# Delta-rule keys kept unnormalised: key norms in biases and factors, decays masked first and exponentiated per head, the first state product held back

## The chip, the cores and the metric

The kernel runs on one core of one Trainium2 chip. The metric is the device time of one execution in microseconds; three executions of the kernel before took 1210.19, 1213.13 and 1214.18 us, so its median is 1213.13 us. One execution was profiled: every duration below is from it, in microseconds from the start of its span. PE is the matrix engine, DVE the vector engine, ACT the scalar engine with the activation tables, POOL the GpSimd engine; SP issues all the transfers (DMAs) spoken of here.

## The reference, cut to what matters

A decoder block of width 1024 over 528 positions (16 learned ones, then 512): SwiGLU, a mixer, SwiGLU. The mixer has an attention branch and a gated delta rule with 8 heads of 64 keys and 64 values. The change touches the delta rule alone:

```python
q = l2norm(q) * (GDN_DK ** -0.5)
k = l2norm(k)                      # k * rsqrt(sum(k*k) + EPS), per position and head
beta = sigmoid(b_raw)
gc = cumsum(g)                     # g < 0: a decay per position and head
decay = exp(where(tri_incl, gc[:, None] - gc[None, :], -inf))
kb = k * beta
lmat = where(tri_strict, (kb @ k.T) * decay, 0)
tmat = inverse(eye + lmat)
u_c, w_c = tmat @ (v * beta), tmat @ (kb * exp(gc))
intra = (q @ k.T) * decay
# per chunk, with the state carried:
v_new = u - w @ state
o = (q * exp(gc)) @ state + intra @ v_new
state = state * exp(g_last) + (k * exp(g_last - gc)).T @ v_new
```

The kernels work on five chunks: chunk 0 is the 16 learned positions, chunks 1 to 4 have 128 positions each.

## The kernel before

All activations lie channels by positions. Weights are streamed by SP into three buffers, split by ACT (`whi`, L173) and DVE (`wlo`, L174) into a high and a low part, and multiplied in three passes (L188). The program is four stages one after the other: SwiGLU 1, the mixer's projections with the delta rule, the attention, SwiGLU 2. Within the mixer each part is given a priority (`At(slot)`), a scheduler puts the instructions of each engine into a fixed order by these, and `HOLD` (L67) adds orderings: an entry `(name, i, t, k)` lets the instructions marked `name, i` come only behind matmul `k` of projection `t`. Each engine then works strictly in its order, so that a waiting instruction holds up all behind it on that engine.

The delta rule's part, in the order in which the data flow:

- `rates` makes beta, the cumulative decays `gc` (token-major), `lb` = gc - log(1 + exp(-b)), that is gc + log(beta), and `kd` = exp(g_last - gc), and writes `gc` as rows to memory (`growd`).
- `k_tile` (four, one for two heads): projection, short convolution on DVE (three instructions L710), SiLU on ACT into `kT`, transposes on PE to token-major (`tok`, L723), and copies into `ktok` with sums of squares `ss`.
- `decay(c, True, n)`, called ahead of `k_norm`: the row of decays is broadcast to all partitions by a DMA, POOL subtracts it from `lb` (L782), POOL masks it (L783) and ACT exponentiates all eight heads in one instruction (L785, recorded at L147).
- `k_norm`: the norm `kn`, five multiplications of `ktok` by it (L747, DVE and POOL), 20 transposes back on PE (L750, `kback`), 20 ACT copies into `kT` (L752), and five multiplications of `ktok` by `kd` on POOL (L753).
- `lower(c)`: eight products of keys (L804, tile `kk`, in two PSUM buffers, the only two of their tag) times the decay on DVE (L806), then to memory (`ld`).
- `v_tile`, `q_tile`, `z_tile`: as `k_tile`; the products L761 and L1252 take beta into `bv`.
- `solve`: the inverse by forward substitution, 31 steps on DVE for chunks 1 to 4 (`lt`, `T`, `rk`, L827 and L829), 15 steps on POOL for chunk 0 (`meta`). `merge_meta` transposes the latter on DVE (L838) into `X[0]`; `merge` puts together the former.
- `scan(c)`: `vn` = X times the right-hand side, an ACT copy of it (L922), the state product `su` of `ktok` and `vn` (L926), and for c > 0 the outputs with `decay(c, False, P)`.

The projections for keys, values and queries (`qkv` in the rows), each of 48 matmuls, run on PE through all this, and their results leave PSUM through two buffers by a DVE instruction (L706, tile `cx`).

Of the kernel before, what the change touches and what calls it, by code (L numbers as in the profile page):

```python
# [41 lines left out]
NTAG = {"tA": 3, "tB": 3, "tC": 3, "tD": 4, "kb": 10, "rr": 1, "vn": 2, "m": 4}  # L42
# [6 lines left out]
    "rr": "rr", "vn": "vn", "m": "tb xt nz nz2 zs meta phm plm",  # L49
# [17 lines left out]
HOLD = (('nm', 0, 0, 32), ('nm', 1, 0, 36), ('b', 0, 1, 36), ('g', 0, 2, 42), ('tok', 1, 4, 5), ('tok', 2, 5, 4), ('tok', 3, 6, 2), ('back', 0, 8, 25), ('tok', 4, 8, 21), ('tok', 7, 10, 0), ('sq', 0, 11, 25), ('kvn', 0, 14, 12), ('kvn', 1, 14, 18))  # L67
# [25 lines left out]
def build(tc, a, out, tap=None):  # L93
# [3 lines left out]
    with ctx:  # L97
# [375 lines left out]
        # ---------------- feed-forward 1  # L473
# [42 lines left out]
        # ---------------- token mixer  # L516
# [91 lines left out]
        # ---- rates and decays, token-major  # L608
        def rates():
# [59 lines left out]
            nc.vector.tensor_tensor(out=lb, in0=gc, in1=lb, op=ALU.subtract)  # L669
            nc.vector.tensor_tensor(out=kd, in0=egl, in1=gc, op=ALU.subtract)  # L670
# [15 lines left out]
        eglp = one([P, 5, 4], "eglp")  # L686

# [13 lines left out]
        # ---- short convolution, token-major copies  # L701
# [33 lines left out]

        def k_norm(psm):
            pm = psm[0:NM].rearrange("p c x -> p (c x)")
            sq = tmp("tsq", SEQ, NM)
            nc.scalar.activation(sq, pm, AF.Square)
            nc.scalar.copy(ktok[0][0:NM], pm)  # L740
            nc.vector.tensor_reduce(out=ss[0:NM, 0], in_=hd(sq), axis=AX.X, op=ALU.add)
            rsqrt(kn, ss, 1.0)
            pst = sm_tile("psmk")
            for c in range(5):
                n, o = tlen(c), toff(c)
                kk = hd(ktok[c][0:n])
# [7 lines left out]
            tap("kT0", kT[0])  # L754

        def v_tile(i, psm):
# [3 lines left out]
            for c in range(1, 5):  # L760
                nc.vector.tensor_tensor(out=hd(bv[c][:, i * P:(i + 1) * P]), in0=hd(ps[:, c - 1]),  # L761
                                        in1=hb(beta[:, c, 2 * i:2 * i + 2], P, 2), op=ALU.mult)
# [11 lines left out]
        # ---- the triangular systems  # L774
        def decay(c, lower, n):
            if lower:
                t = b4("dec", [P, H, P]) if c else one([NM, H, NM], "L0")
            else:
                t = b4("dec", [P, H, P])
            dq.dma_start(t, growd[c, :, 0:n].partition_broadcast(n))  # L780
            gcb = (lb if lower else gc)[0:n, c].unsqueeze(2).broadcast_to([n, H, n])
            nc.gpsimd.tensor_tensor(out=t, in0=gcb if lower else t, in1=t if lower else gcb, op=ALU.subtract)  # L782
            nc.gpsimd.affine_select(out=t, in_=t, pattern=[[0, H], [-1 if lower else 1, n]], compare_op=ALU.is_ge, fill=-BIG,  # L783
                                    base=-1 if lower else 0, channel_multiplier=1 if lower else -1)
            table(t, t, AF.Exp)  # L785
            return t

# [112 lines left out]
        def scan(c):  # L900
# [15 lines left out]
            for h in range(H):  # L916
                if c:
                    nc.tensor.matmul(psv[:, h], lhsT=X[c][:, h], rhs=rr[:, h], start=True, stop=True)
                else:
                    nc.tensor.matmul(psv[0:n, h], lhsT=X[0][0:n, h, 0:n], rhs=bv[0][0:n, h * 64:h * 64 + 64], start=True, stop=True)  # L920
# [553 lines left out]
```

## Time and profile before

| | us |
|---|---|
| median of three executions | 1213.13 |
| the profiled execution's own span | 1213.2 |
| PE busy in it | 1182.6 (97%) |
| DVE busy | 857.0 (71%) |
| ACT busy | 539.7 (44%) |
| POOL busy | 127.1 (10%) |

The span is the profiled execution's whole time. PE's busy time holds its waits on its own pipeline and runs at either of two clock levels, 2.4 GHz (a granted clock of 1.0) or 1.2 GHz (0.5), so the share alone doesn't say where time can be had: the stretches with a low granted clock and the waits do. SwiGLU 1 ends at about 373, the delta rule's part lies between 373 and 640, the attention behind it. A float32 matmul or transpose that isn't split into high and low parts can show two records for each instruction.

### The profile page before, as it was taken

How to read it: one execution, taken by the hardware profiler on the slowest of the kernel's cores; microseconds unless marked ns; L12 is line 12 of the kernel's file. 1: busy time of each engine (PE TensorE's matmuls, PEld its weight loads, DVE VectorE, ACT ScalarE, POOL GpSimd, SP SyncE). 2: the span in 40 equal slices, each digit the busy share in tenths (PEclk: the TensorE clock that was granted, in tenths of full speed). 3: DMA queues.
4: the chain of work that ended last, by engine and by line, in shares of the span. 5: the costliest groups of instructions: out<-in, count | busy, mean ns of one | idle time of the engine just before them, and what ended most of it. 6: DMA issues, size and time to landing. Idle time of an engine off the chain costs nothing.

```text
span 1213.2 us, 20599 instructions
## 1 busy us (share of the span) xinstructions
PE 1182.6 (97%) x8094; PEld 1072.4 (88%) x8094; DVE 857.0 (71%) x1545; ACT 539.7 (44%) x922; POOL 127.1 (10%) x129
## 2 busy tenths in 40 slices
PE   7999999999999899999999999999999999999996
PEld 7999999999999789788897777788889999999985
DVE  7978777876656877784667665554979777786754
ACT  6544334533345553254425564434536433543443
POOL 1000000000011545020400000222000000000002
PEclk9999999999999888898999999999999999999998
DMA  6433233232244322245534544554642233233222
GB/s 233 143 103 100 94 105 105 88 118 75 88 138 138 126 61 81 81 145 149 162 101 142 173 132 135 169 185 141 199 157 88 90 103 104 94 106 115 79 78 70
DMA packets 68961, 145.37 MB, mean 120 GB/s; under 512 B 20000, under 2 KB 26480, under 8 KB 68864
## 3 DMA queue, kind: packets, MB, share of 16 engines
q1 hardware_dynamic: 68320, 143.52, 37.0%
q8 instruction: 64, 1.05, 0.3%
q10 hardware_dynamic: 544, 0.52, 0.1%
q14 instruction: 33, 0.27, 0.1%
HBM read 126.47 MB, written 17.55 MB: 119 GB/s over the span
## 4 chain that ended last, share of the span: by engine, by line
PE 86%; DVE 5%; issue 3%; POOL 2%; ACT 2%; DMA 2%; SPq 0%; DVEq 0%; POOLq 0%; ACTq 0%
PE gu L405 27%; PE dn L188 21%; PE gu L188 11%; PE gate L188 6%; PE wo L188 4%; PE mo L188 3%; PE qkv L188 2%; DVE wlo L174 1%; PE kk L804 1%; PE s L1085 1%; PE s L1082 1%; PE qk L943 1%; POOL rk L827 1%; DVE rk L827 1%; DVE T L829 1%
## 5 line engine op out<-in xcount | busy, mean ns | idle before, releaser
L173 ACT CAST whi<-wraw 128x1024 fp32r<-128x1024 f32 (+1 forms) x127 | 129.2, 1017 | 195.6 <-issue 65.3
L174 DVE TENSOR_TENSOR wlo<-wraw,whi 128x1024 fp32r<-128x1024 f32 (+1 forms) x127 | 155.8, 1227 | 26.2 <-ACT whi L173 25.5
L405 PE MATMUL gu<-hd,form 128*128 128x264 f32 (+1 forms) x1152 | 154.6, 283 | 0.0
L405 PEld LDWEIGHTS gu<-hd,form 128*128 128x128 f32 x1152 | 146.6, 190 | 1.3
L272 ACT CAST form<-sf 128x512 fp32r<-128x512 f32 x128 | 78.6, 620 | 126.1 <-DVE sf L394 67.5
L323 DVE SCALAR_TENSOR_TENSOR hk<-dn,hk 128x528 f32<-128x528 f32 (+2 forms) x49 | 33.7, 688 | 109.8 <-PE dn L188 109.6
L405 PE MATMUL gu<-ut,form 128*128 128x264 f32 x768 | 101.1, 284 | 0.0
L405 PE MATMUL gu<-rb,form 128*128 128x256 f32 x768 | 100.0, 283 | 0.0
L188 PE MATMUL dn<-hd,whi 128*128 128x264 f32 (+2 forms) x366 | 97.4, 319 | 0.0
L272 ACT CAST form<-wraw 128x512 fp32r<-128x512 f32 x96 | 59.3, 620 | 85.2 <-PE gu L405 52.1
L405 PEld LDWEIGHTS gu<-ut,form 128*128 128x128 f32 x768 | 96.5, 188 | 0.0
L405 PEld LDWEIGHTS gu<-rb,form 128*128 128x128 f32 x768 | 95.6, 192 | 0.0
L273 DVE TENSOR_TENSOR form<-sf,form 128x512 fp32r<-128x512 f32 x128 | 86.9, 683 | 11.2 <-ACT form L272 11.1
L188 PE MATMUL gate<-ut,whi 128*128 128x512 f32 x256 | 87.8, 417 | 0.0
L188 PE MATMUL dn<-ra,whi 128*128 128x264 f32 x464 | 85.3, 285 | 0.0
L188 PE MATMUL dn<-ut,whi 128*128 128x512 f32 (+1 forms) x238 | 83.6, 390 | 0.0
L235 POOL TENSOR_TENSOR sqa<-sq 128x512 f32<-128x512 f32 (+1 forms) x3 | 4.5, 1514 | 674.3 <-ACT sq L222 674.3
L188 PE MATMUL gu<-ra,whi 128*128 128x264 f32 x384 | 64.5, 290 | 7.4 <-ACT whi L173 6.6
L188 PE MATMUL dn<-ra,wlo 128*128 128x264 f32 x352 | 71.6, 285 | 0.0
L188 PE MATMUL dn<-ut,wlo 128*128 128x512 f32 (+1 forms) x182 | 70.4, 387 | 0.0
L273 DVE TENSOR_TENSOR form<-wraw,form 128x512 fp32r<-128x512 f32 x96 | 65.5, 684 | 6.7 <-ACT form L272 6.4
L188 PEld LDWEIGHTS dn<-ra,whi 128*128 128x128 f32 x464 | 68.5, 189 | 0.0
(435 smaller groups left out, 2480.7 us busy)
## 6 DMA issues: line engine op xcount, KB each, us to landing
wraw<-w SPq DMA_DIRECT2D x88, 512.0 KB, 3.3
wraw<-win SPq DMA_DIRECT2D x36, 512.0 KB, 3.5
wraw<-d SPq DMA_DIRECT2D x32, 512.0 KB, 3.8
wraw<-d SPq DMA_DIRECT2D x16, 384.0 KB, 3.2
hk<-xT SPq DMA_DIRECT2D x16, 264.0 KB, 3.6
dec<-growd SPq DMA_DIRECT2D x8, 512.0 KB, 5.8
gated<-gt SPq DMA_DIRECT2D x16, 256.0 KB, 2.2
sg<-gated SPq DMA_DIRECT2D x16, 256.0 KB, 2.8
```

Of the source, the lines that this page charges most:

```text
L173: ih = nc.scalar.copy(hi[:, 0:n], raw[:, 0:n])
L174: il = (nc.gpsimd if pool_lo else nc.vector).tensor_tensor(out=lo[:, 0:n], in0=raw[:, 0:n], in1=hi[:, 0:n].bitcast(F32), op=ALU.subtract)
L188: trail.append(nc.tensor.matmul(o, lhsT=w, rhs=x[:, lo_:hi_], start=start and k == 0 and pi == 0, stop=stop and k == n - 1 and pi == 2).ins)
L272: nc.scalar.copy(hi, x)
L273: (eng or nc.vector).tensor_tensor(out=lo, in0=x, in1=hi.bitcast(F32), op=ALU.subtract)
L323: nc.vector.scalar_tensor_tensor(out=o, in0=p, scalar=0.5, in1=o, op0=ALU.mult, op1=ALU.add)
L405: nc.tensor.matmul(ps, lhsT=wt, rhs=xt, start=k == 0 and i == 0, stop=k == 3 and i == 2)
L804: nc.tensor.matmul(ps[0:n, h4, 0:n], lhsT=hs(kT, h, o, o + n), rhs=hs(kT, h, o, o + n), start=True, stop=True)
L827: eng.tensor_tensor(out=tm, in0=lt[:, m + 1:m + 1 + n, m:m + 1].broadcast_to([nl, n, m + 1]), in1=T[:, m:m + 1, 0:m + 1].broadcast_to([nl, ...
L829: eng.tensor_tensor(out=T[:, m + 1:m + 1 + n, 0:m + 1], in0=T[:, m + 1:m + 1 + n, 0:m + 1], in1=tm, op=ALU.subtract)
L943: nc.tensor.matmul(ps[:, h4], lhsT=hs(kT, h, o, o + n), rhs=hs(qT, h, o, o + n), start=True, stop=True)
L1082: nc.tensor.matmul(ps[:, 0:w], lhsT=Q[h][:, b * P:(b + 1) * P], rhs=K[h][:, k0:k1], start=True, stop=True)
```

## The change

The keys in `kT` and `ktok` stay unnormalised. The norm goes into other terms:

- `key_norm` (new, called by `k_norm`) makes `kn` and its logarithm `lk`, with one correction step on both. `lb` gets the logarithm of the row's norm and, since the column's norm is not divided out, of the norm again: `lb` += `lk`, where `lk` is minus twice the half-logarithm. `bkn` = beta times `kn` takes beta's place in `bv`; `nbeg` gets `kn` squared. The 20 transposes, their copies and the ten multiplications of `ktok` are gone.
- `decay` broadcasts and masks the row itself; POOL's subtraction is gone. The exponential comes later, in `powers`, one ACT instruction for each head, with the scale -1 (or 1) and the bias `lb` (or `ngc` = -gc): 40 instructions for the triangular systems (8 of 16x16 and 32 of 128x128), 32 for the outputs.
- `kd` is multiplied into a copy of `vn` on DVE (`vk`, L936 of the new text), ahead of the state product, which reads `vk`. For chunk 0 ACT's copy of `vn` is gone.
- `HOLD` loses `('back', 0, 8, 25)` and gains `('vn', 0, 16, 14)`: the eight `vn` products of chunk 0 come behind matmul 14 of the first `z` projection.
- The scratch space for DMA descriptors is set to 4096 bytes; a tag `vk` with one buffer is added.

```diff
-HOLD = (... ('tok', 3, 6, 2), ('back', 0, 8, 25), ('tok', 4, 8, 21), ('tok', 7, 10, 0), ('sq', 0, 11, 25), ('kvn', 0, 14, 12), ...)
+HOLD = (... ('tok', 3, 6, 2), ('tok', 4, 8, 21), ('tok', 7, 10, 0), ('sq', 0, 11, 25), ('vn', 0, 16, 14), ('kvn', 0, 14, 12), ...)
...
+            nc.vector.tensor_scalar_mul(ngc, gc, -1.0)
...
+        def key_norm():
+            e = epst[:, 0:1]
+            v, y = (one([P, 5, H], "kn" + k) for k in "vy")
+            table(lk, ss, AF.Ln, bias=e, scale=1.0)
+            table(kn, lk, AF.Exp, scale=-0.5)
+            nc.scalar.activation(v, ss, AF.Identity, bias=e, scale=1.0)
+            nc.scalar.activation(y, kn, AF.Square)
+            nc.vector.scalar_tensor_tensor(out=y, in0=y, scalar=-0.5, in1=v, op0=ALU.mult, op1=ALU.mult)
+            nc.vector.scalar_tensor_tensor(out=kn, in0=y, scalar=1.5, in1=kn, op0=ALU.add, op1=ALU.mult)
+            nc.vector.tensor_scalar(y, y, 2.0, 1.0, op0=ALU.mult, op1=ALU.add)
+            nc.vector.tensor_tensor(out=lk, in0=y, in1=lk, op=ALU.subtract)
...
-            rsqrt(kn, ss, 1.0)
-            pst = sm_tile("psmk")
-            for c in range(5):
-                n, o = tlen(c), toff(c)
-                kk = hd(ktok[c][0:n])
-                (nc.vector if c % 2 else nc.gpsimd).tensor_tensor(out=kk, in0=kk, in1=hb(kn[0:n, c], n), op=ALU.mult)
-                ps = sm_tile("kback").rearrange("p (i x) -> p i x", i=4) if c else pst.rearrange("p (i x) -> p i x", i=4)
-                for i in range(4):
-                    mark("back", c, nc.tensor.transpose(out=ps[:, i, 0:n], in_=ktok[c][0:n, i * P:(i + 1) * P], identity=ident[0:n, 0:n]))
-                for i in range(4):
-                    nc.scalar.copy(kT[i][:, o:o + n], ps[:, i, 0:n])
-                nc.gpsimd.tensor_tensor(out=kk, in0=kk, in1=hb(kd[0:n, c], n), op=ALU.mult)
+            key_norm()
+            kn2 = one([P, 5, H], "kn2")
+            nc.vector.tensor_tensor(out=kn2, in0=kn, in1=kn, op=ALU.mult)
+            nc.vector.tensor_tensor(out=bkn, in0=beta, in1=kn, op=ALU.mult)
+            nc.vector.tensor_tensor(out=nbeg, in0=nbeg, in1=kn2, op=ALU.mult)
+            nc.vector.tensor_tensor(out=lb, in0=lb, in1=lk, op=ALU.add)
...
-            gcb = (lb if lower else gc)[0:n, c].unsqueeze(2).broadcast_to([n, H, n])
-            nc.gpsimd.tensor_tensor(out=t, in0=gcb if lower else t, in1=t if lower else gcb, op=ALU.subtract)
-            nc.gpsimd.affine_select(out=t, in_=t, pattern=[[0, H], [-1 if lower else 1, n]], compare_op=ALU.is_ge, fill=-BIG,
-                                    base=-1 if lower else 0, channel_multiplier=1 if lower else -1)
-            table(t, t, AF.Exp)
+            nc.gpsimd.affine_select(out=t, in_=t, pattern=[[0, H], [-1 if lower else 1, n]], compare_op=ALU.is_ge,
+                                    fill=BIG if lower else -BIG, base=-1 if lower else 0, channel_multiplier=1 if lower else -1)
...
+        def powers(t, c, lower, n):
+            for h in range(H):
+                table(t[:, h], t[:, h], AF.Exp, bias=(lb if lower else ngc)[0:n, c, h:h + 1], scale=-1.0 if lower else 1.0)
...
-            vn = hd(tok("vn"))
-            nc.scalar.copy(vn[0:n], psv[0:n])
+            if c:
+                vn = hd(tok("vn"))
+                nc.scalar.copy(vn, psv)
             if c < 4:
+                vk = hd(tok("vk"))
+                nc.vector.tensor_tensor(out=vk[0:n], in0=psv[0:n], in1=hb(kd[0:n, c], n), op=ALU.mult)
...
             k_norm(psm)
             for c in range(5):
+                powers(L[c], c, True, tlen(c))
+            for c in range(5):
                 lower(c)
...
-    nc = bacc.Bacc("TRN2", target_bir_lowering=False, num_devices=1)
+    nc = bacc.Bacc("TRN2", target_bir_lowering=False, num_devices=1, dynamic_dma_scratch_size=4096)
```

The scheduler's orders change at several places. PE before, behind the projection of the second value tile (`psmk` and `kback` are the transposes back, `tok` those of the values, `qkv` a projection):

```order
L188 MATMUL qkv<-ut,whi 128x264 x2
L750 MATMUL psmk<-ident,ktok 128x16 x4
L750 MATMUL kback<-ident,ktok 128x128 x8
L723 MATMUL tok<-ident,vT 128x128 x3
L750 MATMUL kback<-ident,ktok 128x128 x4
L723 MATMUL tok<-ident,vT 128x128
```

PE now, in the projection of the third value tile's surroundings (`kk` are the products of keys of one chunk, two heads for each `kT`):

```order
L188 MATMUL qkv<-ut,whi 128x264 x2
L814 MATMUL kk<-kT_4647 128x128 x2
L814 MATMUL kk<-kT_4648 128x128 x2
L814 MATMUL kk<-kT_4649 128x128 x2
L814 MATMUL kk<-kT_4650 128x128 x2
L188 MATMUL qkv<-ut,whi 128x264 x2
L188 MATMUL qkv<-ut,wlo 128x264 x2
L188 MATMUL qkv<-ut,whi 128x264 x2
```

The transposes back are gone, the key products of chunk 0 are spread singly ahead of this (from the second key tile on), and those of chunks 1 to 4 stand one projection earlier, with 6 to 10 `qkv` matmuls between one chunk's eight and the next.

POOL before, from the key multiplications to the solve of chunk 0 (`T` and `X` are the big tiles of the other chunks, which are cleared here):

```order
L747 TENSOR_TENSOR ktok<-ktok,knorm 128x512 x2
L753 TENSOR_TENSOR ktok<-ktok,kd 16x512
L753 TENSOR_TENSOR ktok<-ktok,kd 128x512 x4
L835 MEMSET meta 32x256
L822 MEMSET T 128x1024
L827 TENSOR_TENSOR rk<-meta 8x15
L852 MEMSET X 128x1024
L823 MEMSET T 128x32
```

POOL now, at the end of chunk 0's solve:

```order
L837 TENSOR_TENSOR rk<-meta 8x28
L839 TENSOR_TENSOR meta<-meta,rk 8x2x14
L837 TENSOR_TENSOR rk<-meta 8x15
L839 TENSOR_TENSOR meta<-meta,rk 8x15
L832 MEMSET T 128x1024
L862 MEMSET X 128x1024
L833 MEMSET T 128x32
```

The clearing of `T` moves from ahead of chunk 0's 30 solve instructions to behind them. In SP's order the solve's result `td` stands ahead of the load of `lt`, as before it did not.

PE before, where the query projections end and the first `z` projection begins:

```order
L188 MATMUL qkv<-ut,wlo 128x264 x2
L920 MATMUL vn<-bv,meta 16x64 x2
L769 MATMUL psq<-pairs,tsq 128x2 x4
L920 MATMUL vn<-bv,meta 16x64 x6
L188 MATMUL z<-ut,whi 128x512 x2
```

PE now, at chunk 0's `vn`:

```order
L188 MATMUL z<-ut,wlo 128x512
L930 MATMUL vn<-bv,meta 16x64 x8
L188 MATMUL z<-ut,whi 128x512 x2
L188 MATMUL z<-ut,wlo 128x512
L188 MATMUL z<-ut,whi 128x512 x2
L188 MATMUL z<-ut,wlo 128x512
L188 MATMUL z<-ut,whi 128x512 x2
L939 MATMUL su<-vk,ktok 128x128
```

All eight `vn` now stand inside the `z` projection, behind its matmul 14, with eight more of it ahead of the state product `su`. On DVE the transpose of `meta` (L838, L848 now) moves from behind the eighth step of the big solve to behind its first.

## Rows read from the trace of the kernel before

**Rows 1.** The page, chain that ended last, shares of the span

```profile
PE 86%; DVE 5%; issue 3%; POOL 2%; ACT 2%; DMA 2%; SPq 0%; DVEq 0%; POOLq 0%; ACTq 0%
```

**Rows 2.** Windows: stretch, length, busy us PE, PEld, DVE, ACT, POOL; PE clock; DMA

```profile
408.40:414.00 5.60, 0.00 (x0) 0.00 (x0) 5.53 (x9) 0.95 (x3) 5.45 (x4) 0.73 0.20 80
414.00:418.30 4.30, 4.29 (x21) 4.21 (x22) 3.40 (x5) 2.43 (x5) 4.06 (x3) 0.55 0.08 12
428.20:463.00 34.80, 32.63 (x223) 29.84 (x222) 23.96 (x44) 12.90 (x37) 12.38 (x10) 0.75 0.17 42
463.00:487.60 24.60, 24.60 (x203) 24.23 (x201) 20.37 (x41) 10.19 (x15) 16.13 (x33) 1.00 0.31 94
487.60:497.40 9.80, 7.71 (x39) 6.09 (x38) 6.38 (x13) 3.48 (x5) 0.00 (x0) 0.65 0.33 108
497.40:521.40 24.00, 23.01 (x108) 18.74 (x108) 20.93 (x45) 5.04 (x7) 4.21 (x3) 1.00 0.27 89
550.90:561.80 10.90, 10.90 (x108) 8.52 (x107) 5.58 (x8) 4.36 (x8) 0.00 (x0) 0.53 0.32 98
603.00:635.00 32.00, 32.00 (x233) 29.16 (x232) 21.26 (x60) 7.69 (x12) 3.54 (x3) 1.00 0.31 104
```

**Rows 3.** Waits of PE, 370 to 640: waiter, releaser, us, times, longest

```profile
PE tok L723 <- ACT kT L147: 5.7, 1, 5.7
PE vn L920 <- DVE meta L838: 2.1, 1, 2.1
PE kk L804 <- DVE L L806: 1.4, 1, 1.4
PE psmk L750 <- POOL ktok L747: 0.7, 1, 0.7
```

**Rows 4.** Timeline of DVE: start, us, line, operation [idle before]

```profile
400.19 0.76 DVE L710 SCALAR_TENSOR_TENSOR kT<-cx,cols,kT 128x528 f32<-128x528 f32 x1
402.50 2.92 DVE L174 TENSOR_TENSOR wlo<-wraw,whi 128x1024 fp32r<-128x1024 f32 x1
405.34 4.11 DVE L710 SCALAR_TENSOR_TENSOR kT<-cx,cols,kT 128x528 f32<-128x528 f32 x1
...
447.39 0.69 DVE L806 TENSOR_TENSOR dec<-kk,dec 128x512 f32<-128x512 f32 x1
...
489.27 0.43 DVE L838 STREAM_TRANSPOSE meta<-meta 32x256 f32<-32x256 f32 x1 [2.95 <-DMA meta<-td]
```

**Rows 5.** POOL's groups by line, 390 to 450: busy, mean ns

```profile
L782 POOL TENSOR_TENSOR dec<-lb,dec 128x1024 f32<-128x1024 f32 x4 | 8.2, 2040 | 21.9 <-DMA dec<-growd 21.9
```

**Rows 6.** Timeline of POOL: a mask, then chunk 0's solve

```profile
405.64 1.08 POOL L783 TENSOR_SCALAR_AFFINE_SELECT dec<-dec 128x1024 f32<-128x1024 f32 x1
...
466.94 0.21 POOL L827 TENSOR_TENSOR rk<-meta 8x15 f32<-8x15 f32 x1 [19.82 <-DMA meta<-ld]
...
470.79 1.17 POOL L827 TENSOR_TENSOR rk<-meta 8x48 f32<-8x48 f32 x1
...
484.61 0.57 POOL L829 TENSOR_TENSOR meta<-meta,rk 8x15 f32<-8x15 f32 x1
```

**Rows 7.** Timeline of PE: transposes back, products of 64 rows at either clock

```profile
438.92 1.31 PE L750 MATMUL kback<-ident,ktok 128*128 128x128 f32 x8
...
449.70 2.67 PE L804 MATMUL kk<-kT 64*128 64x128 f32 x16
...
603.80 1.16 PE L943 MATMUL qk<-qT,kT 64*128 64x128 f32 x8
```

**Rows 8.** Timeline of ACT: two instructions with a bias column, one exponential of before

```profile
431.27 0.31 ACT L147 ACTIVATE knorm<-ss,epst 128x40 f32<-128x40 f32 x1
431.49 0.31 ACT L206 ACTIVATE rsq<-ss,epst 128x40 f32<-128x40 f32 x1
...
582.53 1.06 ACT L147 ACTIVATE dec<-dec 128x1024 f32<-128x1024 f32 x1
```

**Rows 9.** DMA issues: the solve's load, size, us from issue to landing

```profile
lt<-ld SPq DMA_DIRECT2D x1, 512.0 KB, 4.8
```

More of the change, by code (lines that the diff above doesn't have):

```diff
@@ L41 @@
 ROPE = 12.5
-NTAG = {"tA": 3, "tB": 3, "tC": 3, "tD": 4, "kb": 10, "rr": 1, "vn": 2, "m": 4}
+NTAG = {"tA": 3, "tB": 3, "tC": 3, "tD": 4, "kb": 10, "rr": 1, "vn": 2, "vk": 1, "m": 4}
 TAG = {n: t for t, ns in {
@@ L48 @@
     "kb": "ktok bv ph pl yh yl mhl",
-    "rr": "rr", "vn": "vn", "m": "tb xt nz nz2 zs meta phm plm",
+    "rr": "rr", "vn": "vn", "vk": "vk", "m": "tb xt nz nz2 zs meta phm plm",
 }.items() for n in ns.split()}
@@ L66 @@
 CYCLE = (0, 1, 2)
-HOLD = (('nm', 0, 0, 32), ('nm', 1, 0, 36), ('b', 0, 1, 36), ('g', 0, 2, 42), ('tok', 1, 4, 5), ('tok', 2, 5, 4), ('tok', 3, 6, 2), ('back', 0, 8, 25), ('tok', 4, 8, 21), ('tok', 7, 10, 0), ('sq', 0, 11, 25), ('kvn', 0, 14, 12), ('kvn', 1, 14, 18))
+HOLD = (('nm', 0, 0, 32), ('nm', 1, 0, 36), ('b', 0, 1, 36), ('g', 0, 2, 42), ('tok', 1, 4, 5), ('tok', 2, 5, 4), ('tok', 3, 6, 2), ('tok', 4, 8, 21), ('tok', 7, 10, 0), ('sq', 0, 11, 25), ('vn', 0, 16, 14), ('kvn', 0, 14, 12), ('kvn', 1, 14, 18))
 GX = (1,) * 16
@@ L686, in build @@
         eglp = one([P, 5, 4], "eglp")
+        bkn = one([P, 5, H], "bkn")
+        lk = one([P, 5, H], "lk")
+        ngc = one([P, 5, H], "ngc")
         def rope_key():
@@ L761, in v_tile @@
                 nc.vector.tensor_tensor(out=hd(bv[c][:, i * P:(i + 1) * P]), in0=hd(ps[:, c - 1]),
-                                        in1=hb(beta[:, c, 2 * i:2 * i + 2], P, 2), op=ALU.mult)
+                                        in1=hb(bkn[:, c, 2 * i:2 * i + 2], P, 2), op=ALU.mult)
         def q_tile(i, psq):
@@ L919, in scan @@
                 else:
-                    nc.tensor.matmul(psv[0:n, h], lhsT=X[0][0:n, h, 0:n], rhs=bv[0][0:n, h * 64:h * 64 + 64], start=True, stop=True)
-            vn = hd(tok("vn"))
-            nc.scalar.copy(vn[0:n], psv[0:n])
+                    mark("vn", 0, nc.tensor.matmul(psv[0:n, h], lhsT=X[0][0:n, h, 0:n], rhs=bv[0][0:n, h * 64:h * 64 + 64], start=True, stop=True))
+            if c:
+                vn = hd(tok("vn"))
+                nc.scalar.copy(vn, psv)
             if c < 4:
+                vk = hd(tok("vk"))
+                nc.vector.tensor_tensor(out=vk[0:n], in0=psv[0:n], in1=hb(kd[0:n, c], n), op=ALU.mult)
                 pss = tk_tile("su").rearrange("p (i d) -> p i d", i=4)
@@ L926, in scan @@
                     nc.tensor.matmul(pss[:, i], lhsT=ktok[c][0:n, i * P:(i + 1) * P],
-                                     rhs=vn[0:n, 2 * i:2 * i + 2].rearrange("p h d -> p (h d)"), start=True, stop=True)
+                                     rhs=vk[0:n, 2 * i:2 * i + 2].rearrange("p h d -> p (h d)"), start=True, stop=True)
                 for p in range(2):
@@ L938, in scan @@
             e = decay(c, False, P)
+            powers(e, c, False, P)
             pk = [sm_tile("qk").rearrange("p (h s) -> p h s", h=4) for _ in range(2)]
@@ L1252, in build @@
             nc.vector.tensor_tensor(out=hd(bv[0][0:NM]), in0=psm[0:NM].rearrange("p c (h d) -> p (c h) d", d=64),
-                                    in1=hb(beta[0:NM, 0], NM), op=ALU.mult)
+                                    in1=hb(bkn[0:NM, 0], NM), op=ALU.mult)
         psq = ax_tile("psq")
```

1 line of the change is left out of this document (removed).

## The prediction

> **What bounds the kernel now.** I read the chain of waits first: PE carries 86% of it [rows 1]. So time is to be had only where PE stands, where it runs at its lower clock, or where it does work that goes away. The windows and PE's waits between 370 and 640, where all the changed code lies, show both kinds of loss. PE stands four times for longer than half a microsecond at an instruction that this change touches: 5.7 us at the third key tile's transposes, 0.7 at the transposes back, 1.4 at the key products, 2.1 at chunk 0's `vn` [rows 3]. Behind three of them the granted clock is at 1.2 GHz for a while: it averages 0.55 from 414.0 to 418.3, 0.75 from 428.2 to 463.0 and 0.65 from 487.6 to 497.4; a fourth such stretch, 0.53 from 550.9 to 561.8, lies in the first merge [rows 2]. From 603 to 635, where the outputs are made, PE is busy throughout at 1.00 [rows 2]: nothing removed from POOL or added to ACT or DVE there moves the end unless it makes PE wait.
>
> **The third key tile (term A).** PE waits for ACT's SiLU, which waits for DVE's convolution. The last convolution instruction that runs alone takes 0.76 us; the same kind at 405.34 takes 4.11, and the weight split at 402.50 2.92 [rows 4]. Meanwhile POOL subtracts: 8.2 us in four instructions, with a mask of 1.08 behind each [rows 5, 6]. I read it as DVE, with two operands from SBUF, being shut out while POOL works from SBUF. The change takes the subtractions away and leaves the masks: three follow each other as their rows land, 3.2 us, the fourth comes later, its row being loaded behind a weight. A convolution instruction can then lose at most about 3 us at a time where it lost 3.35. The bounds of the gain are nothing (the masks fall exactly on the same instructions and are as much in the way) and 5.7 us of waiting plus (1 - 0.55) x 4.3 = 1.9 of clock. I take 3.0: about 2.7 us of waiting stay, and a wait of 1.4 us was enough for the lower clock further on, so the 1.9 stay too. The key products of chunk 0 now stand just ahead of those transposes and wait for the same SiLU; the wait only changes its name.
>
> **From the second value projection to the fourth (term B), 428.2 to 463.0.** Removed are 16 full transposes back, two times 1.31 = 2.6 us [rows 7], the four small ones and the waits of 0.7 and 1.4 us. ACT's copies and POOL's and DVE's multiplications of `ktok` stood beside other work, except where PE waited for them, which is counted.
>
> New here is that PE's key products wait for the norm. Chunk 0's products occupy both PSUM buffers of their tag until DVE has multiplied them by the decay, which needs `lb` with the norm in it and `powers`. Chunk 1's products and all behind them on PE wait for that. The chain behind the fourth key tile's transposes: squares and their sum, 2.5 us as an estimate from a row of 0.69 for 512 columns [rows 4] and the copies beside it; four ACT instructions at strides of 0.22 [rows 8], 0.9; on DVE three convolution instructions, 2.3, an eviction of 0.7, a weight split of twice a convolution's columns, 1.5, and eight small ones, about 1 [rows 4]; eight 16x16 exponentials at 0.2, 1.6. Together 10.5 us. PE has 89 projection matmuls from there to chunk 1's products; at the pace of 463.0 to 487.6, 24.6 / 203 = 0.121 us [rows 2], 10.8. The two meet at nearly the same moment. I take 0.8 us of new waits in all over the four chunks; the bounds are 0 and, with 2 us of lateness at chunk 1 and 0.4 at each of the others, 3.2.
>
> `powers` replaces one instruction of 1.06 us by eight with a bias column. Two such instructions of 40 columns take 0.31 each and start 0.22 apart; with (1.06 - 0.31) / 984 us for each further column, 128 columns come to 0.38 alone and 0.29 in a train [rows 8]: 2.3 us a chunk, 3.0 if they don't overlap. A chunk's eight products take 2 x 1.16 = 2.3 us at the full clock [rows 7], the projection matmuls between two chunks 0.7 to 1.2 more, so ACT stays ahead, by 0.7 us a chunk in the first case and barely in the second. If that cover goes, each chunk costs PE the difference. The Trainium skill, "ScalarE: Activation LUTs", section "What ACT_TABLE_LOAD costs", speaks against splitting: every activation has a fixed part, a bias column adds to it, and only part of it overlaps with the next. By its figures a 128-column one costs an estimated 0.29 us in a train, which the rows' estimate matches; the sum would be the same by either, and the unsplit price that an eighth of 1.06 would suggest, 0.13, is wrong by both.
>
> The clock: a mean of 0.75 over 34.8 us is 17.4 us at the lower level. Four chunks of products fill 4 x 2.67 = 10.7 of it, and at the full clock would take 2.32 each, which saves 1.4; the other 6.7 us would take half, which saves 3.3. Together 4.7 us, if the clock stays up. It held at 1.00 from 603 to 635 with products of 64 rows between denser matmuls and no gap [rows 2, 7], and fell here behind gaps of 0.7 and 1.4 us; the gaps that I expect are smaller and apart, so I take it as held. Term B: 2.6 + 2.1 - 0.8 + 4.7 = 8.6.
>
> **Chunk 0's state and the hold (term C).** Before 489.27 DVE itself stands 2.95 us at the transpose of `meta` [rows 4], with an eviction queued behind it, because chunk 0's solve on POOL began only at 466.94 and ended at 485.2 [rows 6]. Its load stood in SP's queue behind all the big `ld` transfers; now it stands ahead of them and needs only chunk 0. The solve starts some 30 us earlier, so the transpose finds its data; that, more than the hold, ends the 2.1 us of PE's wait, since a hold alone would leave DVE stuck. It also ends the cause of the lower clock: (1 - 0.65) x 9.8 = 3.4 us. `vk` is one more DVE instruction, about 0.69 us as a product from PSUM [rows 4], and `su` now waits for it behind the DVE steps of the big solve: I take 1.0 us lost. Term C: 2.1 + 3.4 - 1.0 = 4.5. Bounds: 0 if DVE, busy 20.4 of 24.6 and 20.9 of 24.0 us on either side [rows 2], can't follow PE, and 5.5.
>
> **Nothing or unseen.** ACT's 32 exponentials for the outputs cost 4 x (2.3 - 1.06) = 5.0 us more in an engine busy 7.7 of 32.0 [rows 2]; POOL's last four subtractions go from a place where PE doesn't wait; three `vk` there lie on DVE, busy 21.3 of 32. If the cover were gone each `vk` would cost 0.7. For the scratch space and the added tag I take nothing. For the first merge I take nothing either: its products move by about nine gate and value matmuls, and whether its (1 - 0.53) x 10.9 = 5.1 us at the lower clock come back I can't tell; between 0 and 5.1.
>
> **The sum.** 3.0 + 8.6 + 4.5 = 16.1 us off the profiled execution's 1213.2, which lies 0.1 above the median: 1197.1, so 1197. Its own range is 1190 (the merge's 5.1 and 2 more from A) to 1201.
>
> **The rivals.**
> *The clock falls all the same in the key products.* For it: four waits near each other, and `kk` at 64 rows follows each; against it the full clock from 603 to 635. Then B loses 4.7, and with exponentials of 0.38 another 2: 1202 to 1204.
> *DVE becomes the bound.* With PE faster, evictions, the 31 solve steps and `vk` must fit in less time. DVE had 4.2, 3.4 and 3.1 us free in the three stretches from 463 to 521.4 [rows 2], more than the 5.5 that C takes out, but not at the right moments. Then C is lost: 1201.6. With the rival before, 1206 to 1208.
> *The big solve waits for chunk 0's (slower).* DVE's first solve step needs `T` cleared by POOL, now behind chunk 0's 30 instructions, and `lt`, now issued behind their result; the load takes 4.8 us [rows 9]. The solve of chunk 0 took 18.2 us with two clearings in it [rows 6]; I expect it to end about 2 us before DVE arrives, and `lt` about 2 us after. Behind that step on DVE stands the eviction of the next query projection, and PE has two buffers: some 4 us more and each microsecond is PE's. If every one of the 30 instructions were shut out by DVE as the one of 1.17 us was [rows 6], the solve would take 36 us, 18 more: about 15 of waiting and 2 of clock, and C is lost. Then 1213.2 - 3.0 - 8.6 + 17 = 1219. It turns slower from 12 us of waiting on. Against it: 18.2 us for 30 instructions and two clearings is 0.6 each at most, half of 1.17.
> *The change frees PE but its waits only move:* A gives nothing, the key products wait 3 us and drop the clock, C is lost: 1213.2 - 2.6 - 2.1 + 3 = 1211.5.
>
> **How the numbers follow.** The forecast 0.55; the clock 0.20; DVE 0.11; waits that only move 0.08; slower 0.06. A difference of 0.3% (3.6 us) is about what a measurement of this kernel can tell from none: the first three are faster, 0.86; the fourth is the same, 0.08; the fifth slower, 0.06. The range reaches from 1187, three microseconds below the forecast's own range for bubbles that I didn't count, to 1207, the joint case of clock and DVE.
>
> **What would show it.** Right: PE's wait at the third key tile (now at `kk`) between 1 and 4 us; no `kback`; the convolution near 405 under 2.5 us; a granted clock above 0.9 from the first value projection to the last; no wait of DVE at `meta`; `vn` of chunk 0 without idle time ahead of it. Wrong: a wait of several microseconds of PE at `kk` with DVE or ACT as releaser, DVE standing at the first `rk`, a granted clock near 0.75 where the key products are, or time lost behind 640, where I expect the same as before.

## The result, and the profile after

| | before | after |
|---|---|---|
| median, us | 1212.53 (4 executions, 1210.19 to 1214.18) | 1195.77 (4 executions, 1195.21 to 1196.73) |
| ratio, 95% interval | | 0.9866 (0.9849 to 0.9883) |
| span of the profiled execution | 1213.2 | 1193.8 |

The kernel became 16.8 us faster in the median; 1197 was predicted. The two profiled executions lie 19.4 us apart, and it is these that can be compared stretch by stretch; the one of before is a long one (42 of the 46 executions of before that ran beside the experiments have a shorter span), so a part of the 19.4 belongs to that execution. First the waits of PE after the change, between 370 and 640 (waiter, releaser, us, times, longest). They answer to [rows 3]:

```profile
PE yT L982 <- DVE zs L983: 2.9, 2, 1.9
PE z L188 <- DVE z L593: 1.8, 1, 1.8
PE v L1036 <- DVE kn L1027: 1.3, 1, 1.3
PE kk L814 <- ACT kT L147: 1.0, 1, 1.0
...
PE tok L727 <- ACT vT L147: 0.3, 1, 0.3
...
PE kk L814 <- DVE dec L816: 0.2, 1, 0.2
```

The waits of before at `tok`, `vn`, `kk <- DVE L` and `psmk` are gone or down to 1.0; the first three here are new (`yT` are the transposes of the delta rule's outputs, `v` the attention's values). The windows after (length, busy us of PE, PEld, DVE, ACT, POOL, then the granted clock and DMA) answer to [rows 2]:

```profile
403.00:409.70 6.70, 5.71 (x55) 5.23 (x54) 5.97 (x10) 2.54 (x6) 4.41 (x4) 1.00 0.45 164
409.70:416.20 6.50, 6.50 (x57) 6.31 (x57) 4.51 (x9) 3.57 (x7) 0.00 (x0) 1.00 0.24 83
427.70:439.30 11.60, 11.15 (x100) 9.85 (x98) 7.12 (x12) 11.57 (x34) 6.78 (x22) 1.00 0.37 81
439.30:469.20 29.90, 29.84 (x246) 29.55 (x247) 27.19 (x64) 12.87 (x20) 5.62 (x13) 1.00 0.28 94
479.90:483.70 3.80, 3.80 (x11) 2.98 (x10) 3.80 (x9) 0.00 (x0) 0.00 (x0) 0.55 0.46 148
527.20:538.60 11.40, 11.40 (x185) 9.35 (x184) 7.73 (x13) 5.80 (x12) 0.00 (x0) 1.00 0.42 142
619.00:627.00 8.00, 5.10 (x26) 4.20 (x26) 6.71 (x16) 2.19 (x7) 0.00 (x0) 0.79 0.58 181
```

The clock is at 1.00 where it was 0.55, 0.75 and 0.53 in [rows 2]. It falls in a new place, near 480, and at 619 to 627, where PE is busy for 5.1 of 8 us.

To place the 19.4 us I compare when PE reaches the same work in both. PE's timeline after (start, us, line, operation, [idle before]): the fourth key tile's transposes, the four chunks' key products, the transposes of the first and fourth value tiles, two steps of the first merge:

```profile
416.25 0.60 PE L727 MATMUL tok<-ident,kT 128*128 128x128 f32 x4
...
427.80 1.21 PE L814 MATMUL kk<-kT 64*128 64x128 f32 x16
...
429.87 1.75 PE L814 MATMUL kk<-kT 64*128 64x128 f32 x16
...
433.22 1.75 PE L814 MATMUL kk<-kT 64*128 64x128 f32 x16 [0.19 <-DVE dec L816]
...
435.83 1.57 PE L814 MATMUL kk<-kT 64*128 64x128 f32 x16
...
439.36 0.66 PE L727 MATMUL tok<-ident,vT 128*128 128x128 f32 x4 [0.31 <-ACT vT L147]
...
450.75 0.66 PE L727 MATMUL tok<-ident,vT 128*128 128x128 f32 x4
...
527.25 2.11 PE L874 MATMUL z<-xt,dec 32*32 32x32 f32 x64
...
540.62 0.94 PE L905 MATMUL z<-nz,t 64*64 64x64 f32 x13 [0.20 <-DVE nz L902]
```

The same places in PE's timeline before:

```profile
421.95 0.60 PE L723 MATMUL tok<-ident,kT 128*128 128x128 f32 x4
...
468.99 0.66 PE L723 MATMUL tok<-ident,vT 128*128 128x128 f32 x4
...
547.90 2.11 PE L864 MATMUL z<-xt,dec 32*32 32x32 f32 x64 [0.38 <-DVE xt L856]
...
565.35 0.97 PE L895 MATMUL z<-nz,t 64*64 64x64 f32 x13
```

The lead of the changed kernel is 0.1 us at the first key tile's transposes (397.72 and 397.59). The last gate matmul starts at 757.6 before and 737.5 after.

| up to | lead, us | gained since the row above | predicted |
|---|---|---|---|
| fourth key tile's transposes | 5.7 | 5.6 (A) | 3.0 |
| last value transposes | 18.2 | 12.5 (B) | 8.6 |
| first merge | 20.7 | 2.4 (C) | 4.5 |
| behind the first merge's low clock | 24.7 | 4.1 | 0, at most 5.1 |
| last gate matmul | 20.1 | -4.6 | 0 |
| end | 19.4 | -0.7 | 0 |

So the sum came out close because the errors of its terms, up to 4.6 us each, nearly cancel. The experiments ask where each came from.

On DVE, the answers to [rows 4]: the weight split takes 1.21 where it took 2.92, the convolution behind it 1.59 where it took 4.11, and the transpose of `meta` waits for nothing:

```profile
402.39 1.21 DVE L174 TENSOR_TENSOR wlo<-wraw,whi 128x1024 fp32r<-128x1024 f32 x1
403.53 1.59 DVE L714 SCALAR_TENSOR_TENSOR kT<-cx,cols,kT 128x528 f32<-128x528 f32 x1
...
453.64 0.42 DVE L848 STREAM_TRANSPOSE meta<-meta 32x256 f32<-32x256 f32 x1
```

On POOL, the answers to [rows 6]: the first mask, and the first and last step of chunk 0's solve, which takes 11.9 us in all:

```profile
399.52 1.09 POOL L790 TENSOR_SCALAR_AFFINE_SELECT dec<-dec 128x1024 f32<-128x1024 f32 x1 [19.28 <-DMA dec<-growd]
...
430.88 0.21 POOL L837 TENSOR_TENSOR rk<-meta 8x15 f32<-8x15 f32 x1 [21.36 <-DMA meta<-ld]
...
442.59 0.21 POOL L839 TENSOR_TENSOR meta<-meta,rk 8x15 f32<-8x15 f32 x1
```

On ACT, 32 exponentials of `powers` (two trains, with one weight copy between them): 0.30 us each, near the 0.29 estimated from [rows 8]:

```profile
426.95 3.31 ACT L147 ACTIVATE dec<-dec,lb 128x128 f32<-128x128 f32 x11
...
431.11 6.25 ACT L147 ACTIVATE dec<-dec,lb 128x128 f32<-128x128 f32 x21
```

### The profile page after: what moved, and what is told of

It reads as the page before. It is cut to its first block, busy times and chain, and to the rows that moved or that the text cites. A ratio compares the mean times of both kernels' runs of the same rounds, so it can differ in the third digit from the quotient of the medians.

```text
span 1193.8 us, 20601 instructions
## 1 busy us (share of the span) xinstructions
PE 1167.5 (98%) x8074; PEld 1058.5 (89%) x8074; DVE 848.3 (71%) x1554; ACT 548.5 (46%) x964; POOL 93.1 (8%) x112
## 4 chain that ended last, share of the span: by engine, by line
PE 50%; DVE 1%; ACT 0%; issue 0%; DVEq 0%
PE gu L405 13%; PE dn L188 10%; PE gate L188 6%; PE gu L188 6%; PE mo L188 4%; PE wo L188 4%; PE s L1099 1%; PE pt L1138 1%; PE o L1163 1%; PE s L1096 1%; PE qk L957 1%; PE oi L962 1%; PE qn L188 1%; PE o L1158 0%; PE vn L928 0%; DVE hk L1398 0%
## 5 line engine op out<-in xcount | busy, mean ns | idle before, releaser
L174 DVE TENSOR_TENSOR wlo<-wraw,whi 128x1024 fp32r<-128x1024 f32 (+1 forms) x127 | 150.9, 1188 | 26.2 <-ACT whi L173 24.2
L188 PE MATMUL qkv<-ut,whi 128*128 128x264 f32 x384 | 66.1, 289 | 0.0
```

Of the source, the lines that this page charges most:

```text
L174: il = (nc.gpsimd if pool_lo else nc.vector).tensor_tensor(out=lo[:, 0:n], in0=raw[:, 0:n], in1=hi[:, 0:n].bitcast(F32), op=ALU.subtract)
L188: trail.append(nc.tensor.matmul(o, lhsT=w, rhs=x[:, lo_:hi_], start=start and k == 0 and pi == 0, stop=stop and k == n - 1 and pi == 2).ins)
```

## The experiments

The twelve kernels ran in three groups of four, each group on one chip with the kernel before beside it: 1210.59 us in the first group, 1212.09 in the second, 1210.70 in the third (medians; single executions of before range from 1206.7 to 1218.9). Times of different groups are compared by their ratios to it. A ratio with its interval isn't the quotient of the two medians, and the two differ by up to 0.26%, about 3 us; so what an experiment did is read from its trace first, and a difference of that size between groups isn't read from the times.

### A subtraction put back on POOL

`zz` is a tile of zeros.

```diff
 def decay(c, lower, n):
+            if lower:
+                nc.gpsimd.tensor_tensor(out=t, in0=t, in1=zz[0:n, c].unsqueeze(2).broadcast_to([n, H, n]), op=ALU.subtract)
```

> The changed kernel with a subtraction put back on POOL ahead of each mask of the triangular systems: it subtracts a column of zeros, so the values stay, and the order of the instructions on PE, DVE, ACT and SP stays word for word that of the changed kernel. Theory (POOL's subtraction, working from SBUF, shuts DVE out of the third key tile's convolution): PE's wait at kk near 408, 1.0 us in the changed kernel, grows to 4 to 6 us, a convolution instruction of DVE there takes about 4 us, the clock falls behind the wait and takes 1 to 2 us more: 1201 to 1203 us. Rival (the 5.7 us of before came from the order of the work there, not from the subtraction): the wait stays near 1 us, 1195 to 1197 us.

Measured: 1200.92 us (1199.05 to 1201.26), 0.9899 of before (0.9855 to 0.9943). Its waits of PE, then the convolution on DVE:

```profile
PE kk L819 <- ACT kT L147: 3.0, 1, 3.0
...
PE tok L727 <- ACT kT L147: 0.5, 1, 0.5
```

```profile
404.53 2.71 DVE L714 SCALAR_TENSOR_TENSOR kT<-cx,cols,kT 128x528 f32<-128x528 f32 x1
```

The wait grows by 2.5 us to 3.5, the convolution from 1.59 to 2.71, both less than expected, and the clock averages 0.84 and 0.81 over the two 5-us windows from 410: 1.75 us. The fourth key tile's transposes start at 420.56 where the changed kernel has them at 416.25. The theory holds, with 4.3 us of the 5.6.

### The subtraction taken out of the kernel before

```diff
-            nc.gpsimd.tensor_tensor(out=t, in0=gcb if lower else t, in1=t if lower else gcb, op=ALU.subtract)
+            if not lower:
+                nc.gpsimd.tensor_tensor(out=t, in0=t, in1=gcb, op=ALU.subtract)
```

> The kernel before without POOL's subtraction in the triangular systems, that is with exponentials of the bare row of decays instead of the decays; all else, and the order of the instructions on PE, DVE, ACT and SP, is word for word that of the kernel before. Theory (the subtraction alone makes term A): PE's wait at the third key tile falls from 5.7 to between 1 and 2.5 us, the clock stays at 1.0 behind it, the fourth key tile's transposes stand 4 to 6 us earlier; the lower clock at the key products (445 to 462 in before, now some 5 us earlier) remains, since the waits at the transposes back and at kk remain; in all 5 to 6 us less than the kernel before. Rival (the masks and the weight split are as much in the way): the wait stays above 4 us and the time within 2 us of before.

Measured: 1206.60 us (1202.10 to 1209.64), 0.9968 of before (0.9950 to 0.9986). The wait, and POOL's first mask:

```profile
PE tok L723 <- ACT kT L147: 2.3, 1, 2.3
```

```profile
402.24 1.30 POOL L784 TENSOR_SCALAR_AFFINE_SELECT dec<-dec 128x1024 f32<-128x1024 f32 x1 [21.87 <-DMA dec<-growd]
```

The wait shrinks by 3.4 us and 2.3 stay, near the 2.7 that the prediction expected to stay; the clock fell behind it all the same (0.70 over 410 to 415), which the expectation had wrong. The fourth key tile's transposes start at 418.41, 3.5 us earlier than before, where 4 to 6 were expected. What the changed kernel has over this one is the start of the first mask: 399.52 against 402.24. In SP's order after, the first row of decays is loaded ahead of a weight, and before behind it; so the first mask is out of the way when the convolutions come. That is a second cause. No run moved that load alone, but the four kernels give both causes both ways: the wait is 5.7 with the subtraction and the late row (before), 3.5 with the subtraction and the early row (the experiment above), 2.3 without it and late, 1.0 without it and early (after). The Trainium skill, "SBUF — State Buffer", section "Who interferes with whom", says that a DVE instruction with two SBUF inputs contends with a POOL instruction that reads SBUF, through a port pair that only one of them can hold at a time. Both runs agree: the convolution takes 2.71 and 2.93 us near 404.5, 1.59 after, 4.11 before, and 0.76 where POOL does nothing [rows 4].

### The hold and the early solve, each way round

Without the new hold, and with the load of chunk 0's system late (`stores` collects the stores of the big systems):

```diff
-('sq', 0, 11, 25), ('vn', 0, 16, 14), ('kvn', 0, 14, 12)
+('sq', 0, 11, 25), ('kvn', 0, 14, 12)
```

> The changed kernel without the new hold on chunk 0's vn; the vn products then stand about 4 us earlier, around the first two z matmuls and the queries' psq, everything else in the same order. Theory (the early solve of chunk 0 ends the wait, the hold is worth little): no wait at vn, 1195 to 1197 us; the fall of the clock near 480, which lies behind vn, psq and su standing together, may weaken and give back up to 1.7 us. Rival (the hold carries the gain): PE waits about 2 us at vn, the clock falls behind it, 1199 to 1201 us.

```diff
-            dq.dma_start(lt, ld)
+            ins = dq.dma_start(lt, ld).ins
+            if w != 32:
+                behind(ins, stores[-1])
```

> The changed kernel with the load of chunk 0's system put behind the last store of the big systems in SP's order, as it stood before the change; the hold stays. Theory (the early load is what frees DVE, as the prediction said): the solve on POOL ends late, DVE stands at the transpose of meta and PE at vn, 1199 to 1201 us. Rival (the whole chain of the key products ends 23 us earlier, so that even the late load is early enough): the solve begins near 445 and ends by 465, vn at 474 finds its data, 1195 to 1198 us.

Measured: 1198.99 us (1196.56 to 1201.95), 0.9883 of before (0.9843 to 0.9924); and 1197.45 us (1195.32 to 1197.92), 0.9866 (0.9828 to 0.9904). In neither does PE wait at `vn`. Without the hold the clock stays up near 480, and the last `z` matmul starts at 500.0, with it at 500.3. Its median stands at the lower end of the rival's range all the same; the profiled execution is its fastest, the others have lower mean clocks, and where they lose isn't seen. With the late load DVE does stand at the transpose, and nobody behind it is late:

```profile
463.76 0.43 DVE L851 STREAM_TRANSPOSE meta<-meta 32x256 f32<-32x256 f32 x1 [1.78 <-DMA meta<-td]
```

The theory of the late load falls: `vn` starts at 474.9, 11 us later. So in these traces the changed kernel needs neither part against the wait, since the key products end 23 us earlier (437.4 and 460.6).

The kernel before with the hold alone, and with the early load alone (the second is the edit above turned round, `behind(stores[0], ins)`):

> The kernel before with the new hold on chunk 0's vn alone (behind matmul 14 of the first z projection), the solve of chunk 0 as late as before. Theory of the prediction (a hold alone leaves DVE stuck at the transpose of meta until 489): the wait of 2.1 us at vn goes, since vn comes some 4 us later, but DVE stands as long, 2.9 us, and what is queued behind it makes PE wait elsewhere; 0 to 2 us gained. Rival (the hold is what ends the wait): no wait of PE over 0.5 us from 480 to 500, the clock stays up, 4 to 5 us gained.

> The kernel before with the load of chunk 0's system put ahead of the big systems' stores in SP's order, and no hold. The order changes with it in the first merge and the outputs too, so that only the stretch up to 520 is read. Theory of the prediction (the early solve ends the wait): the solve on POOL begins 15 to 25 us earlier than 467, DVE doesn't stand at the transpose of meta, PE doesn't wait at vn, and the clock from 487 to 497 is above 0.9: 4 to 5 us gained there. Rival: the wait stays, 2 us, or turns into one at another tile.

Measured: 1207.38 us (1205.41 to 1213.68), 0.9975 of before (0.9956 to 0.9993); and 1206.07 us (1204.08 to 1212.66), 0.9954 (0.9933 to 0.9975). The transpose on DVE with the hold alone, then with the early load alone:

```profile
487.22 0.43 DVE L838 STREAM_TRANSPOSE meta<-meta 32x256 f32<-32x256 f32 x1 [2.82 <-DMA meta<-td]
```

```profile
476.65 0.42 DVE L841 STREAM_TRANSPOSE meta<-meta 32x256 f32<-32x256 f32 x1
```

From the last value transposes to the last `z` matmul, start to start, it takes 52.2 us before, 50.6 with the hold (PE waits 1.4 for an eviction of `z` and 1.2 at `psq`, the queries' norms, instead), 48.7 with the early load (no wait at `vn`; the clock is 0.83 from 486 to 496). In these traces the early load is worth 3.5 us and the hold 1.6, as the prediction ranked them; the intervals of the whole times overlap.

### The first merge's clock

The run with the hold alone has PE's first merge in the order of before, with the same waits ahead of it (0.6 and 0.4 us; 0.5 and 0.4 in before). The first 13.1 us from the merge's start there, then without the subtraction, whose PE order is that of before throughout, and then in before:

```profile
543.90:557.00 13.10, 13.10 (x203) 10.64 (x203) 8.84 (x14) 8.50 (x20) 0.95 (x1) 1.00 0.50 164
```

```profile
545.20:558.30 13.10, 13.08 (x202) 10.65 (x202) 8.91 (x14) 8.51 (x20) 0.95 (x1) 1.00 0.48 158
```

```profile
547.90:561.00 13.10, 13.10 (x151) 10.55 (x152) 8.21 (x13) 7.17 (x16) 0.00 (x0) 0.62 0.30 105
```

The same order ran at 1.00 twice and at 0.62 once. So the 4.1 us gained in the merge are not the change's: they belong to the execution of before that was profiled.

### The outputs' transposes

The rows above show `yT` waiting 2.9 us. In the changed order two of its four groups stand next to each other, in one PSUM buffer, with 7 gate matmuls between the last `oi` and the first `yT`; before there were 22.

```diff
+YT = ((1, 24), (2, 29), (3, 32), (4, 38))
+        for c, k in YT:
+            for ins in marks["yT", c]:
+                behind(ins, gsteps[k])
```

> The changed kernel with holds on the last transposes of the delta rule's outputs (yT): the four groups are put behind gate matmuls 24, 29, 32 and 38 of the attention's gate steps, so that no two stand back to back. Theory (the changed kernel lost 2.9 us of waiting at yT and some 1.7 us of clock behind it, since the order put two groups of them next to each other while one PSUM buffer holds them): both come back, 1191 to 1192 us. Rival (DVE is late there whatever PE does, and the wait only moves to the next instruction that needs it): 1195 to 1196 us.

Measured: 1195.12 us (1194.25 to 1197.05), 0.9852 of before (0.9814 to 0.9890). The rival is right, the wait moved to the attention's transposes `pt`:

```profile
PE pt L1139 <- DVE pl L1148: 2.7, 1, 2.7
```

DVE is late there: between 616.4 and 620.4 of this run it multiplies the outputs by their norms and splits a weight, and everything else queues behind. So the next run gives DVE time instead of moving one wait:

```diff
+        behind(marks["s", 0][0], gsteps[28])
```

> The changed kernel with the first scores of the attention held behind matmul 28 of its gate steps, so that 12 more gate matmuls stand ahead of them and the yT groups have gate matmuls and scores between them, as they had in the kernel before. Theory (DVE is late at yT because the scores' evictions come ahead of the outputs' normalisation, while PE has run out of gate matmuls that need no DVE): the 2.9 us at yT fall under 1, the clock near 625 stays up, 3 to 5 us less than the changed kernel, 1191 to 1193 us. Rival (the wait only moves again, as with the holds on yT): 1194 to 1197 us.

Measured: 1192.46 us (1192.01 to 1194.87), 0.9861 of before (0.9827 to 0.9894). Its windows there; the mean clock of each is 1.00:

```profile
615.00:620.00 5.00, 5.00 (x29) 4.14 (x28) 3.89 (x14) 2.80 (x12) 0.00 (x0) 1.00 0.65 213
620.00:625.00 5.00, 5.00 (x30) 3.94 (x29) 4.13 (x13) 2.31 (x7) 0.00 (x0) 1.00 0.59 173
```

PE no longer stands at `yT`, and the profiled span is 1189.4. The theory holds in the trace, and all four times lie below all ten of the changed kernel on other chips (1195.21 at the least); the ratio lies within the changed kernel's interval and doesn't show the gain.

### A version that beats both

The changed kernel again, then two versions with the hold on the scores (28 and 36) and one more order, an eviction of `z` ahead of the scan's first `rr` (chunk 1's right-hand side) on DVE:

```diff
+        behind(marks["rr", 1][0], marks["ze", 1][0])
```

> The changed kernel itself once more, beside the next three on one chip. 1195 to 1197 us. Its clock should not fall in the first merge (527 to 545); near 480 it may or may not (it fell in two of the five traces in which that stretch has this order or nearly this order), which is worth 1.7 us of the span.

> The changed kernel with the hold on the first scores (behind matmul 28 of the gate steps, as the experiment before) and one more order: DVE evicts the second z projection ahead of the first rr. Theory (PE's wait of 1.8 us near 493 is for that eviction alone, which stands on DVE behind eight rr and eight steps of the solve although its data is ready 7 us earlier): the wait goes, the yT waits stay gone: 1 to 2 us less than with the hold on the scores alone, 1190 to 1191 us. Rival (DVE is full there and the wait moves to the next projection or to vn): 1192 to 1193 us.

> As the one before with the first scores held behind matmul 36 of the gate steps instead of 28. Theory: eight more gate matmuls ahead of the scores give DVE 1.9 us more, and the last waits of the outputs' stage go: 0 to 1 us less. Rival (the gate matmuls are missing later, beside the softmax): 1 to 2 us more.

Measured: 1197.46 us (1196.39 to 1198.83), 0.9888 of before (0.9857 to 0.9919); 1190.37 us (1188.97 to 1196.21), 0.9840 (0.9808 to 0.9872); 1192.18 us (1191.69 to 1196.45), 0.9855 (0.9824 to 0.9886). The changed kernel came half a microsecond above its range; its clock fell near 480 and not in the merge. The wait at `z` is gone in both versions, and the one with 28 is 7.1 us below the changed kernel in the median, on the same chip. With 36, PE waits 1.1 us for the softmax instead, so the rival is right there. The profiled execution of the version with 28 is its slowest, and loses its time in the first merge:

```profile
526.00:541.00 15.00, 14.63 (x181) 11.69 (x180) 8.81 (x14) 7.69 (x18) 0.00 (x0) 0.66 0.41 130
```

(1 - 0.66) x 15 = 5.1 us; four of its other five executions have spans 5 to 7 us shorter. The one with 36 shows the same 0.66 there, and four of its other five have spans 4 us shorter. So the fall seems to come in some executions of these versions too. Their order of PE in the merge is a new one, though; whether it favours the fall no run tells.

### The transposes back

```diff
             key_norm()
+            for c in range(5): ... nc.tensor.transpose(out=ps[:, i, 0:n], in_=ktok[c][0:n, i * P:(i + 1) * P], identity=ident[0:n, 0:n])
```

> The changed kernel with the 20 transposes of the keys back put in again on PE, into PSUM, read by nobody; the keys stay unnormalised. The scheduler puts them in one block behind the fourth key tile, and chunk 0's eight products behind them in one block. Theory (term B's 2.6 us are work of PE and nothing else, and it was the waits that took the clock down at the key products): the fourth value tile's transposes come 2.6 to 3.2 us later than in the changed kernel, and the granted clock stays at 1.0 in the key products. Rival (the transposes themselves, thin work on PE, take the clock down): a clock near 0.5 to 0.75 for some microseconds behind them and 5 to 8 us lost.

Measured: 1203.36 us (1199.00 to 1205.30), 0.9934 of before (0.9911 to 0.9956). The transposes and the first two chunks' products:

```profile
419.97 1.97 PE L764 MATMUL kback<-ident,ktok 128*128 128x128 f32 x16
...
427.72 1.26 PE L820 MATMUL kk<-kT 64*128 64x128 f32 x16
...
429.83 1.74 PE L820 MATMUL kk<-kT 64*128 64x128 f32 x16
```

The clock stays at 1.00 from 419.6 to 440, so the transposes don't take it down in this execution, and they cost 2 us of PE in a block. The last value transposes come only 1.2 us later than in the changed kernel's second trace (452.30 and 451.12), less than either theory: chunk 0's products, in one block here, cost less too. The whole is 5.9 us slower in the median, with a new wait of 2.8 us at `psq` and, in all other executions, a lower mean clock than in the profiled one; where it falls there isn't seen. As a price for the transposes the time is inconclusive.

## Why the prediction was right, point by point

**The time.** 1195.77 against 1197, by the forecast's own case: less waiting, and the clock held through the key products. Of its signs, the wait at `kk` (1.0), the convolution near 405 (1.59), the clock from the first to the last value projection (1.00), `meta` and `vn` all came as stated. Of the signs against it one came: time was lost in the outputs, at `yT`, which stands behind 640 in before. That the number came so near is in part luck. The terms' errors, 2.6, 3.9, -2.1, 4.1, -4.6 and -0.7 in the table's order, add up to 3.2. And the sum starts from a span, 1213.2, that it sets beside a median of times; in the executions of before that list both, the time is 1.7 to 3.3 us longer than the span. So the profiled execution was slower than the median one by some 2 to 4 us, which fits the 19.4 us between the spans and the 16.8 between the medians.

**Term A, 5.6 and not 3.0.** The mechanism is right: 3.5 to 4.3 us are the subtraction's, in both directions. The step that failed is "three follow each other as their rows land": the rows land earlier, since a load moved in SP's order past a weight. Only 1.0 us of waiting stayed where 2.7 were expected, and the clock didn't fall behind it.

**Term B, 12.5 and not 8.6.** The mis-sized number is "2 x 1.16 = 2.3 us at the full clock" for a chunk's eight products, taken from `qk` [rows 7]. They take 1.21, 1.75, 1.75 and 1.57, together 6.3 where the forecast's 4 x 2.32 is 9.3. The nearer row was that of `kk` itself [rows 7]: its 2.67 were taken at a granted clock of 0.50, so that half of it, 1.34, would have been the better guess. In the run with the hold alone, whose PE order there is that of before, the last chunk's products ran at 1.00 and took 1.49. (Chunk 1's in before, at 445.28, took 3.53 and not 2.67.) The window of before, then that row:

```profile
449.70:452.30 2.60, 2.60 (x18) 2.38 (x17) 0.31 (x1) 0.00 (x0) 0.00 (x0) 0.50 0.19 32
```

```profile
457.29 1.49 PE L804 MATMUL kk<-kT 64*128 64x128 f32 x16
```

The size of the products is 3.0 of the 3.9 missing; 0.3 more are waits (0.5 for 0.8), and part of the rest is chunk 0's products, which take about 0.7 us and now stand in A's stretch, so that A's real gain is larger and B's smaller by that. The exponentials were sized right, at 0.30 us. The 12.5 are those of one pair of executions: between the same two places before takes 47.0 us, the run with the hold alone 44.1 and that with the early load alone 46.3, with PE's order of before up to there and a granted clock of 0.75, 0.85 and 0.80 over the 34.8 us; both traces of the changed kernel take 34.5. So B is 9.6 to 12.5. That the clock falls in the key products is no chance of one trace: it does in all four traces with the order of before, and in none of the ten with that of the change.

The rows differ in their neighbours: an odd and an even head lie in the two halves of one `kT`, partitions 0 to 63 and 64 to 127. In the order, chunk 1's products alternate halves (1.21 for 16 records), those of the other chunks do so in part (1.57 to 1.75), and a row of `qk` is four products of one half alone, with other work behind it (1.16 for 8 records). Where the changed kernel runs both fours of `qk` in one block, the half changes once and 16 records take 1.71:

```profile
572.37 1.71 PE L957 MATMUL qk<-qT,kT 64*128 64x128 f32 x16 [0.29 <-ACT X L906]
```

So doubling one row of eight counted too much. The Trainium skill, "TensorEngine Tiling (Array Packing)", section "Key Properties", says that different tiles of the array can load weights and multiply in parallel; these rows agree. No run changed that order alone.

**Term C, 2.4 and not 4.5.** The early load and the hold rank as stated, and the wait and the low clock of before, 5.5 us, are gone. What ended them is another thing than the forecast said, though: in the changed kernel the wait stays away without the hold, and also with the late load, since the key products end 23 us earlier; no run left out both at once. And `su` didn't wait (1.0 was taken); instead PE waits 1.8 us for an eviction of `z`, whose data was ready 7 us earlier while DVE did the scan's `rr` and the solve, and the clock is 0.55 for 3.8 us near 480, 1.7 us. The 1.8 us are the rival of the busy DVE, in small. The stretch's other waits gave 0.6 back: 1.3 us came at `v` ahead of the merge, while 1.0 at `z` for a weight and 0.9 ahead of the merge went.

**The merge, 4.1, left open at 0 to 5.1.** It belongs to one execution of before and not to the change.

**The outputs, -4.6 and not 0.** "Nothing removed from POOL or added to ACT or DVE there moves the end unless it makes PE wait" was right, and I then read PE's busy time of before as if its order stayed, in a window (603 to 635) that ends ahead of the `yT` transposes. The order after leaves 7 gate matmuls where 22 stood, and DVE, which had been hidden, was in the way: 2.9 us of waits and (1 - 0.79) x 8 = 1.7 of clock.

The slower rival didn't come near: the solve on POOL took 11.9 us, not 36, and DVE's first solve step waited for nothing.

## What to carry to other kernels

A duration is taken from the same instruction in the same neighbourhood, at its own clock: a row of the same shape in another order was off by a third, and the instruction's own row at the lower clock, halved, would have been nearer. Where a scheduler writes the order, a stage that the change doesn't touch is still to be compared row by row, for the filler that stood between two waits may have moved. And before a low clock is booked as a gain, look at whether the same order shows it in a second execution.

## What the hardware showed that was not expected

The clock's fall is no fixed property of an order. After waits of 1.0, 1.3 and 1.8 us (409.0, 525.2, 494.9 in the changed kernel) it stayed at 1.00; at 480 it fell with PE busy throughout, behind products of 16 rows and of two columns (`vn`, `psq`, `su`). Seven traces have the same order of PE there: it fell in four (both of the changed kernel and those of the last two versions) and not in the other three (the subtraction put back, the spread `yT`, the hold on the scores alone). In the first merge the same order ran at 1.00 twice and at 0.62 once. The total moves with it: in 25 executions of the kernel before on one chip the span goes from 1204.5 us at a mean clock of 0.989 to 1214.1 at 0.981.
